# Sixteen transposes in a row: regrouping the softmax transposes and score matmuls of a hybrid attention block

## The chip, the cores and the metric

One core of a Trainium2 chip runs the whole program. The metric is device time in microseconds (us) per execution, smaller is better. Engines named below: PE (TensorE, matmuls; PEld are its weight loads), DVE (VectorE), ACT (ScalarE), SP (which issues the DMAs). Each engine runs its own instructions strictly in the order in which they stand, and waits on semaphores for the others.

## The reference

One layer of a diffusion backbone over 512 latent tokens of width 1024 and 256 context tokens, all in 32-bit floats. After modulation and RMSNorm one large input projection feeds a gated short convolution and a neighbourhood attention of 16 heads of width 64; both branches are projected, merged through sigmoid gates, projected again, normalised and added to `x`. The part that the change touches is the attention:

```
s_nb  = einsum(q_r, k_win) * scale + bias      # window of keys around each query
s_ctx = einsum(q_r, k_ctx) * scale             # all 256 context keys
p     = softmax(concatenate([s_nb, s_ctx]))
out   = einsum(p_nb, v_win) + einsum(p_ctx, v_ctx)
```

## The kernel before

**Precision.** Every fp32 operand is split into a high part H (rounded to the matmul's fp32r format) and a low part L = x - H; a product is made of two or three matmuls (`split`, L67 to L71: ACT writes H, DVE writes L). A *unit* (`unit`, L227) is one 128x512 output of the input projection: 24 matmuls on PE. Units of values (`proj_N`) and of context (`proj_c`) are 16 matmuls each.

**The attention stage** runs over 8 pairs of heads, 2 heads a pair, 4 blocks of 128 queries a head: 64 blocks. For each block `scores` (L540) makes 128 x 512 scores in one PSUM bank (2 to 4 matmuls, L551 or L560), DVE adds the bias and takes the row maximum (L567) and negates it (L571), ACT takes the exponential and its row sum (L574) into a tile `pt`, DVE inverts the sum (L575) and scales `pt` (L576). PE then turns `pt` by four 128x128 transposes into another bank (`turn2`, L579, matmuls at L583), and ACT and DVE split that into TH and TL (L70, L71). When all four blocks of a head are turned, `gather` (L587, 12 matmuls at L599) multiplies by the values; ACT copies half of the result to `tmp` (L604), and DVE adds it into `attn` (L605, L606).

**Fill.** PE has far more to do in this stage than attention: `plan` (L162) gives each pair a list of projection work, 6 to 8 pieces of about one unit or two value units each: queries and keys of the next pair (`keys_queries`: a unit of queries with rotary embedding, a unit of keys, the context's keys), values, convolution, gates. The loop from L664 spreads these pieces evenly over the pair's eight blocks. DVE and ACT evacuate each piece: `rope` (L481 to L490), the query splits (L516, L518), the key splits (L527, L528), the weight splits (tile `w`, L70, L71, two of each per chunk of weights).

**Order and banks.** In a pass of the loop come: the fill, at block 0 the `gather` of the head before, the scores of the block that is two further on, and at every second block the transposes of two blocks, 8 in a row. Scores rotate over PSUM banks 3 and 4, transposes over 5 and 6, gathers use 7, fill units 0 to 2 (L474, L659). The framework's scheduler keeps mostly to this order, but may pull single instructions forward.

Of the kernel before, what the change touches and what calls it, by code (L numbers as in the profile page):

```python
# [9 lines left out]
F32 = mybir.dt.float32  # L10
# [5 lines left out]
P = 128  # L16
D = 1024
KT = 8
S = 512
C = 256  # L20
EPS = 1e-6
NPAIR = 8
# [5 lines left out]
def layer(ctx: ExitStack, tc, xp, ctxt, cc, wmod, small, wfirst, win, wout, wo, rel, tab, out):  # L28
# [5 lines left out]
    cv = ctx.enter_context(tc.tile_pool(name="cv", bufs=2))  # L34
# [20 lines left out]
    def pairs(tag, n, dtype=F32R):  # L55
        t = [hp.tile([P, 2, n], dtype, name=f"{tag}{k}") for k in range(KT)]
        return t, ([x[:, 0] for x in t], [x[:, 1] for x in t])
# [6 lines left out]
    _, hx = pairs("h", S)  # L64
    hcs, hc = pairs("hc", C)

    def split(H, L, src, scale=None):  # L67

        if scale is None:
            nc.scalar.copy(H, src)  # L70
            nc.vector.tensor_sub(L, src, H.bitcast(F32))  # L71
        else:
            nc.scalar.mul(H, src, scale)
            nc.vector.scalar_tensor_tensor(
                out=L, in0=src, scalar=scale, in1=H.bitcast(F32), op0=ALU.mult, op1=ALU.subtract
            )
# [156 lines left out]
    with ExitStack() as p0:  # L233
# [8 lines left out]
        tps = Banks(6, 7)  # L242
# [228 lines left out]
    aw = pa.enter_context(tc.tile_pool(name="aw", bufs=2, reuse_waits="tile"))  # L471
    swap = [(i + 16) % 32 for i in range(32)]
    lo, hi = slice(0, 64), slice(64, P)
    psS, psT, psO = Banks(3, 4), Banks(5, 6), Banks(7)  # L474
    bt = aw.tile([P, 5, 256], F32, name="bt", bufs=1)
    nc.vector.memset(bt[:, 4], 0.0)
    V, KQ = {}, {}
# [62 lines left out]
    def scores(p, h, b):  # L540
        qd, qe, ks = KQ[p]
        if b == 0:
            nc.sync.dma_start(bt[:, 2 * h:2 * h + 2], rel[p, h])
        s = psS()
        qs = slice(b * P, (b + 1) * P)
        if b < 3:

            t = ks[h][:, b * P:(b + 2) * P]
            kt = bass.AP(t.tensor, t.offset, [t.ap[0], [(4 - b) * P, 2], [1, 2 * P]])
            for n, lhs in enumerate((qd[h], qe[h])):  # L550
                nc.tensor.matmul(  # L551
                    s.rearrange("p (a c) -> p a c", a=2), lhsT=lhs[:, qs], rhs=kt, start=n == 0, stop=n == 1
                )
        else:
            kt = ks[h].rearrange("p (t c) -> p t c", c=P)
            s4 = s.rearrange("p (t c) -> p t c", c=P)
            n = 0
            for lhs in (qd[h], qe[h]):
                for o, i in ((slice(0, 2), slice(0, 4, 3)), (slice(2, 4), slice(4, 6))):
                    nc.tensor.matmul(  # L560
                        s4[:, o], lhsT=lhs[:, qs], rhs=kt[:, i], start=n == 0, stop=n == 3, skip_group_check=True
                    )
                    n += 1
        e = 2 * h + (b == 3)
        m = aw.tile([P, 1], F32, name="m", bufs=4)
        s3 = s.rearrange("p (a c) -> p a c", a=2)
        nc.vector.tensor_tensor_reduce(  # L567
            out=s3, in0=s3, in1=bt[:, e::4 - e][:, 0:2], scale=1.0, scalar=-3.0e38,
            op0=ALU.add, op1=ALU.max, accum_out=m,
        )  # L570
        nc.vector.tensor_scalar(out=m, in0=m, scalar1=-1.0, scalar2=None, op0=ALU.mult)  # L571
        pt = aw.tile([P, S], F32, name="pt", bufs=3)
        z = aw.tile([P, 1], F32, name="z", bufs=4)
        nc.scalar.activation(pt, s, AF.Exp, bias=m, scale=1.0, accum_out=z)  # L574
        nc.vector.reciprocal(z, z)  # L575
        nc.vector.tensor_scalar(out=pt, in0=pt, scalar1=z, scalar2=None, op0=ALU.mult)  # L576
        return pt

    def turn2(pts, b, TH, TL):  # L579
        tps = [psT().rearrange("p (c q) -> p c q", c=4) for _ in pts]  # L580
        for tp, pt in zip(tps, pts):
            for c in range(4):
                nc.tensor.transpose(tp[:, c], pt[:, c * P:(c + 1) * P], ident)  # L583
        for n, tp in enumerate(tps):
            split(TH[:, b + n], TL[:, b + n], tp)

    def gather(p, h, TH, TL):  # L587
        r, q = (lo, hi)[h], (hi, lo)[h]
        o = psO()
        o3 = o.rearrange("p (b q) -> p b q", b=4)  # L590

        work = [(4, slice(0, 4), lambda t: t[:, :, 2]), (5, slice(0, 4), lambda t: t[:, :, 3])]
        work.append((0, slice(0, 4, 3), lambda t: t[:, 0:4:3, 0]))
        for k in range(1, 3):
            work.append((k, slice(k - 1, k + 1), lambda t, k=k: t.rearrange("p b c q -> p (b c) q")[:, 4 * k - 3:4 * k + 1:3]))
        work.append((3, slice(2, 4), lambda t: t[:, 2:4, 1]))
        for n, (kt, dst, src) in enumerate(work):
            for t in (TH, TL):
                nc.tensor.matmul(  # L599
                    o3[:, dst], lhsT=V[p][:, kt, h], rhs=src(t),  # L600
                    start=n == 0 and t is TH, stop=n == len(work) - 1 and t is TL,
                )
        tmp = aw.tile([P, S], F32, name="tmp", bufs=1)
        nc.scalar.copy(tmp[r], o[q])  # L604
        nc.vector.tensor_add(attn[p][r, 64:512], o[r, :448], tmp[r, :448])  # L605
        nc.vector.tensor_add(attn[p][r, 0:64], o[r, 448:], tmp[r, 448:])  # L606
# [29 lines left out]
    def chain(*gs):  # L636
        for g in gs:
            yield from g
# [10 lines left out]
    fill = []  # L649
# [7 lines left out]
            }[name](i))  # L657
        fill.append(f)
    pj.tags = (0, 1, 2)  # L659
    blocks = [(p, h, b) for p in range(NPAIR) for h in range(2) for b in range(4)]  # L660
    pts = {n: scores(*blocks[n]) for n in range(2)}
    T = None
    done = 0
    for i, (p, h, b) in enumerate(blocks):  # L664
        slot = i % 8
        if slot == 0:
            items = chain(*(g for g, _ in fill[p]))
            total, done = sum(n for _, n in fill[p]), 0
        upto = -(-total * (slot + 1) // 8)
        while done < upto:  # L670
            next(items)
            done += 1
        if T is not None and b == 0:
            gather(*T)
        if i + 2 < len(blocks):
            pts[i + 2] = scores(*blocks[i + 2])
        if b == 0:
            TH = aw.tile([P, 4, 4, P], F32R, name="TH", bufs=1)
            TL = aw.tile([P, 4, 4, P], F32R, name="TL", bufs=1)
            T = p, h, TH, TL  # L680

        if b % 2:
            turn2([pts.pop(i - 1), pts.pop(i)], b - 1, TH, TL)
    gather(*T)
    for _ in gate2(3):
        pass
# [23 lines left out]
    for j in range(KT):  # L710
        w = chunk()
        g = G[j]
# [9 lines left out]
        if j == 5:  # L722

            gpost = bp.tile([P, D], F32, name="gpost")
            for i in range(2):
                gb = cv.tile([P, S], F32, name="ta")
                ps = pj()
                for k in range(4):
                    n = 4 * i + k
# [147 lines left out]
```

## Time and profile before

| | |
|---|---|
| median of 3 runs | 731.56 us (730.94 to 731.61) |
| the profiled execution | 731.4 us, its span 729.6 us |
| granted TensorE clock, mean | 0.999 |
| PE busy | 718.8 us (99%) |
| DVE busy | 513.9 us (70%) |
| ACT busy | 332.6 us (46%) |
| transposes L583 | 256, mean 272 ns each from start to end |
| scores' exponentials L574 | 64, mean 693 ns each |

The span is from the first to the last instruction of the profiled execution. Matmuls are pipelined: the next starts before the last has ended, so what one costs is the distance between starts, not its duration. The attention stage lies between 139 and 516 us of the span.

### The profile page before, as it was taken

The page shows a single profiled execution, that of the slowest core. Times are in us where ns is not written, and L with a number is a line of the kernel's source. Part 1 is how long each engine was busy: PE and PEld are TensorE (multiplying, and loading weights), DVE is VectorE, ACT ScalarE, POOL GpSimd, SP SyncE. Part 2 cuts the span into 40 slices and gives each one's busy share as a digit, 9 for nine tenths or more (in the row PEclk, how much of TensorE's full clock was granted, in tenths as well). Part 3 has the DMA queues.
Part 4 walks back from the last instruction along what each step waited for, and adds up shares of the span by engine and source line. Part 5 has one row for each costly group of instructions (what it writes and reads, how often), then busy time and mean ns, then how long its engine had stood idle before and what let it go on. Part 6 is the DMA issues. An engine that isn't in the chain of part 4 may idle for free.

```text
span 729.6 us, 9373 instructions
## 1 busy us (share of the span) xinstructions
PE 718.8 (99%) x3526; PEld 603.3 (83%) x3526; DVE 513.9 (70%) x1057; ACT 332.6 (46%) x619; POOL 0.7 (0%) x6
## 2 busy tenths in 40 slices
PE   7999999999999999999999999999999999999996
PEld 4888888888888888888888888888888888888886
DVE  6979999796998968879879779675753324334423
ACT  6565433563565544654546436434723213314321
POOL 0000000000000000000000000000000000000000
PEclk9999999999999999999999999999999999999999
DMA  8966873213122122122322212222132232234503
GB/s 344 405 244 206 306 263 106 88 55 118 58 73 73 64 81 74 58 74 71 116 73 73 72 59 73 85 77 84 58 115 90 85 115 93 81 116 154 192 2 114
DMA packets 25678, 85.57 MB, mean 117 GB/s; under 512 B 2977, under 2 KB 3361, under 8 KB 25634
## 3 DMA queue, kind: packets, MB, share of 16 engines
q1 hardware_dynamic: 25490, 84.79, 33.8%
q8 instruction: 27, 0.44, 0.2%
q10 hardware_dynamic: 144, 0.20, 0.1%
q14 instruction: 17, 0.14, 0.1%
HBM read 82.88 MB, written 2.10 MB: 116 GB/s over the span
## 4 chain that ended last, share of the span: by engine, by line
PE 94%; DVE 2%; ACT 1%; DMA 1%; SPq 0%; issue 0%; DVEq 0%; ACTq 0%
PE ps L115 20%; PE ps L117 20%; PE ps L116 20%; PE ps L128 6%; PE ps L754 6%; PE ps L599 4%; PE ps L583 4%; PE ps L132 3%; PE ps L551 3%; PE ps L140 2%; PE ps L315 2%; PE ps L319 2%; PE ps L316 2%; DMA wm<-in_wmod 1%; PE ps L560 1%; PE ps L144 1%
## 5 line engine op out<-in xcount | busy, mean ns | idle before, releaser
L115 PE MATMUL ps<-h,w 128*128 128x512 f32 x528 | 207.7, 393 | 0.0
L117 PE MATMUL ps<-h,w 128*128 128x512 f32 x528 | 205.9, 390 | 0.0
L116 PE MATMUL ps<-h,w 128*128 128x512 f32 x528 | 205.8, 390 | 0.0
L71 DVE TENSOR_TENSOR w<-raw,w 128x1024 fp32r<-128x1024 f32 (+1 forms) x98 | 113.3, 1173 | 61.4 <-ACT w L70 61.2
L70 ACT CAST w<-raw 128x1024 fp32r<-128x1024 f32 (+1 forms) x98 | 96.7, 1017 | 85.2 <-PE ps L117 65.7
L117 PEld LDWEIGHTS ps<-h,w 128*128 128x128 f32 x528 | 99.1, 188 | 20.9
L116 PEld LDWEIGHTS ps<-h,w 128*128 128x128 f32 x528 | 99.2, 188 | 20.1
L115 PEld LDWEIGHTS ps<-h,w 128*128 128x128 f32 x528 | 99.2, 188 | 20.0
L574 ACT ACTIVATE pt<-ps,m 128x512 f32<-128x512 f32 x64 | 44.3, 693 | 59.5 <-DVE m L571 59.5
L567 DVE CUSTOM_DVE_ANT_1 ps<-ps,bt 128x512 f32<-128x512 f32 x56 | 38.6, 700 | 15.1 <-PE ps L551 12.0
L71 DVE TENSOR_TENSOR TL<-ps,TH 128x512 fp32r<-128x512 f32 x64 | 42.7, 680 | 5.2 <-ACT TH L70 5.2
L128 PE MATMUL ps<-w,h 128*128 128x512 f32 x128 | 45.2, 395 | 0.0
L70 ACT CAST TH<-ps 128x512 fp32r<-128x512 f32 x64 | 35.0, 588 | 6.6 <-PE ps L583 6.4
L714 DVE SCALAR_TENSOR_TENSOR g<-g,ps 128x512 f32<-128x512 f32 x16 | 11.0, 686 | 37.6 <-PE ps L117 37.6
L632 ACT ACTIVATE g<-ps 128x512 f32<-128x512 f32 x16 | 9.6, 598 | 59.3 <-PE ps L117 59.3
L132 PE MATMUL ps<-w,h 128*128 128x256 f32 x128 | 36.0, 281 | 0.0
L583 PE MATMUL ps<-ident,pt 128*128 128x128 f32 x256 | 33.3, 272 | 0.0
L576 DVE TENSOR_SCALAR pt<-pt,z 128x512 f32<-128x512 f32 x64 | 30.8, 482 | 1.0
L583 PEld LDWEIGHTS ps<-ident,pt 128*128 128x128 f32 x256 | 29.4, 140 | 2.2
L516 ACT ACTIVATE qd<-ta 64x512 fp32r<-64x512 f32 x32 | 20.2, 631 | 22.4 <-DVE ta L490 14.2
L599 PE MATMUL ps<-TH,V 128*128 128x256 f32 (+1 forms) x96 | 28.5, 319 | 0.0
L128 PEld LDWEIGHTS ps<-w,h 128*128 128x128 f32 x128 | 24.0, 187 | 5.3
(156 smaller groups left out, 1192.5 us busy)
## 6 DMA issues: line engine op xcount, KB each, us to landing
raw<-in_win SPq DMA_DIRECT2D x74, 512.0 KB, 4.3
wm<-in_wmod SPq DMA_DIRECT2D x34, 512.0 KB, 7.1
raw<-in_wout SPq DMA_DIRECT2D x16, 512.0 KB, 4.3
bt<-in_rel SPq DMA_DIRECT2D x16, 256.0 KB, 2.6
raw<-in_wo SPq DMA_DIRECT2D x8, 512.0 KB, 4.9
fraw<-in_wfirst SPq DMA_DIRECT2D x8, 384.0 KB, 8.2
x<-in_xp SPq DMA_DIRECT2D x4, 512.0 KB, 5.1
xr<-in_xp SPq DMA_DIRECT2D x4, 512.0 KB, 6.9
```

Of the source, the lines that this page charges most:

```text
L70: nc.scalar.copy(H, src)
L71: nc.vector.tensor_sub(L, src, H.bitcast(F32))
L115: nc.tensor.matmul(ps, lhsT=H[:, k, cs], rhs=mH[k], start=k == 0, stop=False)
L116: nc.tensor.matmul(ps, lhsT=H[:, k, cs], rhs=mL[k], start=False, stop=False)
L117: nc.tensor.matmul(ps, lhsT=L[:, k, cs], rhs=mH[k], start=False, stop=k == KT - 1)
L128: nc.tensor.matmul(ps, lhsT=mH[k][:, ts], rhs=both[:, k].rearrange("p a c -> p (a c)"), start=k == 0, stop=False, skip_group_check=True,)
L132: nc.tensor.matmul(ps[:, :256], lhsT=mL[k][:, ts], rhs=H[:, k], start=False, stop=k == KT - 1, skip_group_check=True)
L567: nc.vector.tensor_tensor_reduce(out=s3, in0=s3, in1=bt[:, e::4 - e][:, 0:2], scale=1.0, scalar=-3.0e38, op0=ALU.add, op1=ALU.max, accum_o ...
L574: nc.scalar.activation(pt, s, AF.Exp, bias=m, scale=1.0, accum_out=z)
L583: nc.tensor.transpose(tp[:, c], pt[:, c * P:(c + 1) * P], ident)
L599: nc.tensor.matmul(o3[:, dst], lhsT=V[p][:, kt, h], rhs=src(t), start=n == 0 and t is TH, stop=n == len(work) - 1 and t is TL,)
L754: nc.tensor.matmul(ps, lhsT=mm[m][k][:, ts], rhs=w[k][:, cols], start=k + o == 0, stop=k == KT - 1 and o == 2)
```

## The change

All four blocks of a head are now turned in one row of 16 transposes, over four PSUM banks, two of which are the scores' own (banks 3 and 4). Scores are no longer made two blocks ahead: in each head come one piece of fill, the `gather` of the head before, the scores of blocks 0 and 1, one piece of fill, the scores of blocks 2 and 3, the rest of that head's fill, and then the 16 transposes. `pt` has four buffers in place of three, and the `tmp` of `gather` comes from a pool of two buffers that the rotary embedding, the convolution and the gates use too.

```diff
-    psS, psT, psO = Banks(3, 4), Banks(5, 6), Banks(7)
+    psS, psT, psO = Banks(4, 3), Banks(4, 5, 6, 3), Banks(7)
...
-        pt = aw.tile([P, S], F32, name="pt", bufs=3)
+        pt = aw.tile([P, S], F32, name="pt", bufs=4)
...
-    def turn2(pts, b, TH, TL):
+    def turn(pts, TH, TL):
+
         tps = [psT().rearrange("p (c q) -> p c q", c=4) for _ in pts]
...
-        for n, tp in enumerate(tps):
-            split(TH[:, b + n], TL[:, b + n], tp)
+        for b, tp in enumerate(tps):
+            split(TH[:, b], TL[:, b], tp)
...
-        tmp = aw.tile([P, S], F32, name="tmp", bufs=1)
+        tmp = cv.tile([P, S], F32, name="tb")
...
-    blocks = [(p, h, b) for p in range(NPAIR) for h in range(2) for b in range(4)]
-    pts = {n: scores(*blocks[n]) for n in range(2)}
...
-    for i, (p, h, b) in enumerate(blocks):
...
-        if T is not None and b == 0:
-            gather(*T)
-        if i + 2 < len(blocks):
-            pts[i + 2] = scores(*blocks[i + 2])
-        if b == 0:
+    for p in range(NPAIR):
+        items = chain(*(g for g, _ in fill[p]))
+        total = sum(n for _, n in fill[p])
+        for h in range(2):
+            def run(n):
+                for _ in range(n):
+                    next(items)
+
+            run(1)
+            if T is not None:
+                gather(*T)
+            pts = [scores(p, h, b) for b in (0, 1)]
+            run(1)
+            pts += [scores(p, h, b) for b in (2, 3)]
+            run((total + 1 - h) // 2 - 2)
             TH = aw.tile([P, 4, 4, P], F32R, name="TH", bufs=1)
             TL = aw.tile([P, 4, 4, P], F32R, name="TL", bufs=1)
             T = p, h, TH, TL
-
-        if b % 2:
-            turn2([pts.pop(i - 1), pts.pop(i)], b - 1, TH, TL)
+            turn(pts, TH, TL)
```

PE in the first head of pair 3, before: the scores of block 3 (ps_2765), then the eight transposes of blocks 0 and 1 (pt_2614, pt_2625), then the context's keys (ps_2792).

```order
L560 MATMUL ps_2765<-ks_2296,qd_2254 128x256 x2
L560 MATMUL ps_2765<-ks_2296,qe_2256 128x256 x2
L583 MATMUL ps_2778<-ident_71,pt_2614 128x128 x4
L583 MATMUL ps_2779<-ident_71,pt_2625 128x128 x4
L140 MATMUL ps_2792<-hc0_88,w_2522 128x512
```

The same head in the change: the scores of blocks 2 and 3, the context's keys (ps_2776) and two value units (the last is ps_2835) behind them, then the row of transposes.

```order
L551 MATMUL ps_2752<-ks_2283,qd_2231 128x512
L551 MATMUL ps_2752<-ks_2283,qe_2233 128x512
L560 MATMUL ps_2763<-ks_2283,qd_2231 128x256 x2
L560 MATMUL ps_2763<-ks_2283,qe_2233 128x256 x2
...
L132 MATMUL ps_2835<-w_2625,h7_87 128x256
L584 MATMUL ps_2861<-ident_71,pt_2695 128x128 x4
L584 MATMUL ps_2862<-ident_71,pt_2706 128x128 x4
L584 MATMUL ps_2863<-ident_71,pt_2758 128x128 x4
L584 MATMUL ps_2864<-ident_71,pt_2771 128x128 x4
```

Blocks 2 and 3 now have the context's keys and two value units between their scores and their transposes; before, a block's scores stood two blocks ahead of the loop, and blocks 0 and 1 alone were turned here.

DVE in that same head, before: from the negated maximum of block 3 (m_2770) over the splits of TL, the sum of the rotary embedding of the keys (ta_2755), the scaling of the block (pt_2773), to the key splits (ks).

```order
L571 TENSOR_SCALAR m_2770<-m_2770 128x1
L71 TENSOR_TENSOR TL_2723<-ps_2778,TH_2722 128x512
L486 TENSOR_TENSOR ta_2755<-ta_2755,tb_2757 128x512
L575 RECIPROCAL z_2774<-z_2774 128x1
L71 TENSOR_TENSOR TL_2723<-ps_2779,TH_2722 128x512
L576 TENSOR_SCALAR pt_2773<-pt_2773,z_2774 128x512
L151 TENSOR_TENSOR ta_2809<-ta_2809,ps_2792 128x256
L528 TENSOR_TENSOR ks_2728<-ta_2755,ks_2728 64x512
L528 TENSOR_TENSOR ks_2729<-ta_2755,ks_2729 64x512
L528 TENSOR_TENSOR ks_2728<-ta_2809,ks_2728 64x256
L528 TENSOR_TENSOR ks_2729<-ta_2809,ks_2729 64x256
```

And in the change, from the maximum of block 3 (ps_2763) to the scalings of blocks 2 and 3 (pt_2758, pt_2771):

```order
L567 ISA ps_2763,m_2768<-ps_2763,bt_1041 128x512
L567 ISA m_2768 128x1
L486 TENSOR_TENSOR ta_2742<-ta_2742,tb_2744 128x512
L571 TENSOR_SCALAR m_2768<-m_2768 128x1
L151 TENSOR_TENSOR ta_2793<-ta_2793,ps_2776 128x256
L71 TENSOR_TENSOR w_2804<-raw_2800,w_2804 128x4x256
L528 TENSOR_TENSOR ks_2715<-ta_2742,ks_2715 64x512
L528 TENSOR_TENSOR ks_2716<-ta_2742,ks_2716 64x512
L575 RECIPROCAL z_2759<-z_2759 128x1
L575 RECIPROCAL z_2772<-z_2772 128x1
L528 TENSOR_TENSOR ks_2715<-ta_2793,ks_2715 64x256
L576 TENSOR_SCALAR pt_2758<-pt_2758,z_2759 128x512
L576 TENSOR_SCALAR pt_2771<-pt_2771,z_2772 128x512
```

The two scalings now stand behind a weight split and three of the four key splits; before, the one scaling stood ahead of them, and the weight split further back.

PE in the first head of pair 1, in the change: the end of the context's keys (ps_1886), the transposes of blocks 0 and 1 (pt_1805, pt_1816), then 26 matmuls of value units (ps_1951, ps_1975), and the transposes of blocks 2 and 3 in their midst.

```order
L144 MATMUL ps_1886<-hc7_95,w_1611 128x256
L584 MATMUL ps_1912<-ident_71,pt_1805 128x128 x4
L584 MATMUL ps_1913<-ident_71,pt_1816 128x128 x4
L128 MATMUL ps_1951<-w_1735,h0_80 128x512
...
L132 MATMUL ps_1975<-w_1735,h4_84 128x256
L584 MATMUL ps_1914<-ident_71,pt_1868 128x128 x4
L584 MATMUL ps_1915<-ident_71,pt_1881 128x128 x4
L128 MATMUL ps_1975<-w_1735,h5_85 128x512
```

In that head the row of 16 is split in two by the scheduler, since only the context's keys remain as fill behind the scores of blocks 2 and 3.

## Rows read from the trace of the kernel before

**Rows 1.** Busy time by engine in the attention stage (stretch, length, busy and count).

```profile
139.00:516.00 377.00, 376.61 (x1966) 321.35 (x1965) 302.81 (x714) 193.35 (x393) 0.00 (x0) 1.00 0.23 75
```

**Rows 2.** What PE waited for in that stage (total, times, longest, us).

```profile
PE ps L551 <- ACT pt L574: 0.4, 1, 0.4
```

**Rows 3.** Timeline of PE, 311 to 325 us (start, duration, instruction, count).

```profile
311.71 1.03 PE L583 MATMUL ps<-ident,pt 128*128 128x128 f32 x8
312.50 0.48 PE L115 MATMUL ps<-h,w 128*128 128x512 f32 x1
312.82 0.40 PE L116 MATMUL ps<-h,w 128*128 128x512 f32 x1
...
315.13 0.39 PE L117 MATMUL ps<-h,w 128*128 128x512 f32 x1
...
318.53 0.39 PE L115 MATMUL ps<-h,w 128*128 128x512 f32 x1
...
323.97 0.39 PE L551 MATMUL ps<-ks,qd 128*128 128x512 f32 x1
```

**Rows 4.** Timeline of PE around its one wait of the stage.

```profile
202.18 0.40 PE L128 MATMUL ps<-w,h 128*128 128x512 f32 x1
202.97 0.50 PE L551 MATMUL ps<-ks,qd 128*128 128x512 f32 x1 [0.39 <-ACT pt L574]
```

**Rows 5.** Timeline of ACT there.

```profile
202.72 0.19 ACT L574 ACTIVATION_READ_ACCUMULATOR pt<-ps,m 128x1 f32 x1
```

**Rows 6.** Timeline of PE, first head of pair 3: gather, scores, context, values, transposes.

```profile
278.48 0.39 PE L599 MATMUL ps<-TH,V 128*128 128x512 f32 x1
...
280.34 0.40 PE L551 MATMUL ps<-ks,qd 128*128 128x512 f32 x1
...
287.52 0.48 PE L140 MATMUL ps<-hc,w 128*128 128x512 f32 x1
...
290.43 0.40 PE L551 MATMUL ps<-ks,qd 128*128 128x512 f32 x1
...
296.44 0.39 PE L551 MATMUL ps<-ks,qd 128*128 128x512 f32 x1
...
296.91 0.60 PE L583 MATMUL ps<-ident,pt 128*128 128x128 f32 x4
```

**Rows 7.** Timeline of DVE in the same head.

```profile
278.68 0.69 DVE L481 TENSOR_TENSOR ta<-ps,cosin 128x512 f32<-128x512 f32 x1 [0.63 <-PE ps L117]
...
283.78 0.70 DVE L567 CUSTOM_DVE_ANT_1 ps<-ps,bt 128x512 f32<-128x512 f32 x1
...
284.62 0.15 DVE L571 TENSOR_SCALAR m<-m 128x1 f32<-128x1 f32 x1
...
285.82 0.49 DVE L576 TENSOR_SCALAR pt<-pt,z 128x512 f32<-128x512 f32 x1
286.46 0.69 DVE L481 TENSOR_TENSOR ta<-ps,cosin 128x512 f32<-128x512 f32 x1 [0.15 <-PE ps L117]
...
290.59 0.68 DVE L71 TENSOR_TENSOR TL<-ps,TH 128x512 fp32r<-128x512 f32 x1
291.19 0.68 DVE L486 TENSOR_TENSOR ta<-ta,tb 128x512 f32<-128x512 f32 x1
...
292.45 0.48 DVE L576 TENSOR_SCALAR pt<-pt,z 128x512 f32<-128x512 f32 x1
292.84 0.41 DVE L151 TENSOR_TENSOR ta<-ta,ps 128x256 f32<-128x256 f32 x1
293.29 2.31 DVE L528 TENSOR_TENSOR ks<-ta,ks 64x512 fp32r<-64x512 f32 x4
295.62 0.70 DVE L567 CUSTOM_DVE_ANT_1 ps<-ps,bt 128x512 f32<-128x512 f32 x1
...
296.24 1.22 DVE L71 TENSOR_TENSOR w<-raw,w 128x1024 fp32r<-128x1024 f32 x1
297.38 0.15 DVE L571 TENSOR_SCALAR m<-m 128x1 f32<-128x1 f32 x1
```

More of the change, by code (lines that the diff above doesn't have):

```diff
@@ L659, in layer @@
     pj.tags = (0, 1, 2)
-    blocks = [(p, h, b) for p in range(NPAIR) for h in range(2) for b in range(4)]
-    pts = {n: scores(*blocks[n]) for n in range(2)}
     T = None
-    done = 0
-    for i, (p, h, b) in enumerate(blocks):
[L665 to L672, printed above, removed]
-        if T is not None and b == 0:
-            gather(*T)
-        if i + 2 < len(blocks):
-            pts[i + 2] = scores(*blocks[i + 2])
-        if b == 0:
+    for p in range(NPAIR):
[12 more added lines that the diff above has]
+            run((total + 1 - h) // 2 - 2)
             TH = aw.tile([P, 4, 4, P], F32R, name="TH", bufs=1)
```

## The prediction

> **What bounds the kernel now.** I read the busy time by stage first: in the attention stage, where the whole change lies, PE is busy for 376.61 of 377.00 us at a granted clock of 1.00, DVE for 302.81, ACT for 193.35 [rows 1]. So PE's stream of matmuls is the time, and any other engine counts only where it makes PE wait. The waits come next: PE waits once there, 0.4 us [rows 2]. As busy PE may still lose time between starts, I read the starts last. In a plain unit 24 matmuls take 318.53 to 323.97, 5.44 us or 0.227 each [rows 3]; that is the pitch to which the rest is held. The change issues the same matmuls and the same evacuations. It can shorten the time only by what PE loses at the borders between kinds of matmul and in that wait, and lengthen it without limit where PE must wait for `pt`.
>
> **Borders of the transposes.** Eight transposes last 1.03 us from the first start to the last end, one lasts 0.27 (the table), so seven steps take 0.76, 0.11 each. From the first transpose to the second matmul behind them is 311.71 to 312.82, 1.11 us: eight times 0.11 and one matmul of 0.227 make 1.11. Changing over is thus free. The ten matmuls behind run at 0.231 (312.82 to 315.13), 0.04 us over plain pitch [rows 3]. A run of transposes costs some 0.04 us beyond its work. The order has 33 such runs before and 17 in the change: 16 x 0.04 = 0.65 us gone.
>
> **Borders of the scores.** Two matmuls of a block's scores take 0.47 us (296.44 to 296.91) [rows 6] against 0.454 at plain pitch: 0.016 a run, and no more than that behind it. The order has 57 runs of scores before, 33 in the change: 24 x 0.02 = 0.45 us. Together 1.1 us, bounds 0 (if the lag belongs to the transposes themselves, whose number stays) and 1.5.
>
> **The one wait.** At 202.18 a matmul starts and the next only at 202.97, where 0.23 would do: 0.56 us; the matmul after comes about 0.1 late as well. The score matmul waited for its bank, until the exponential's row sum ended at 202.72 + 0.19 = 202.91, and started 0.06 us later [rows 4, 5]. In the change, scores follow each other in pairs with a unit between, so this wait goes: 0.66 us.
>
> **What is late next: `pt` of blocks 2 and 3.** In the first head of pair 3 the last scaling before its transposes starts at 292.45 and ends at 292.93; its four transposes start at 296.91 + 4 x 0.11 = 297.35 [rows 6, 7]. So the cover was 4.4 us. In the change, both later blocks lie one stretch behind their scores. In each first head of pairs 0 to 6 that stretch also holds the query and key work of the next pair, so I lay PE and DVE side by side from the end of the query unit (time 0; 278.48 in the trace).
>
> PE: gather 1.86 (278.48 to 280.34), two pairs of scores 0.94, unit 5.44, scores 0.94, context's keys 2.82 (287.52 to 290.43 is 2.91, of which 0.09 belongs to the transposes ahead), one more unit 5.44 (value units 290.90 to 296.44, 5.54) [rows 6, 3]. Transposes start at 17.44; block 2 is due after eight of them at 18.32, block 3 at 18.76 (0.1 later in pairs 3 and 5).
>
> DVE, in its new order, by distances between starts [rows 7]: the rotary embedding of the queries starts at 0.20; with the sums into `attn` and the query split it takes 5.10 (278.68 to 283.78): 5.30. Two bias sums at 0.62 (295.62 to 296.24): 6.54. From a negation to its scaling 1.20 (284.62 to 285.82): 7.74; the second exponential is 0.69 long and lies behind the first, so the second scaling starts at 8.42, and the next instruction 0.40 later: 8.82. The start of the keys' embedding, a bias sum, the second query split, a product and a negation take 4.13 (286.46 to 290.59): 12.95. The second bias sum 0.62: 13.57. Sum of the embedding and small ones, 290.59 to 292.45 without the two TL splits of 0.60 that have moved: 0.66, and one negation more, 0.07: 14.30. The context's sum 0.45 (292.84 to 293.29): 14.75. A weight split 1.14 (296.24 to 297.38): 15.89. Three of the four key splits: of 2.31 I give the last and short one 0.44, so 1.87: 17.76. An inversion 0.07: 17.83. Scaling of block 2 to 18.32, of block 3 to 18.71. With the 0.06 of rows 5: 18.38 and 18.77.
>
> So `pt` comes at 18.38 where PE is due at 18.32. The cover of 4.4 us has shrunk to nothing, within the error of the sum. For pairs 2 to 6 I take 0.1 us of wait each: 0.5. In pair 1 only the context's keys stand behind the scores; the order puts 26 value matmuls ahead of blocks 2 and 3: 17.44 - 5.44 + 0.88 + 26 x 5.54 / 32 + 0.09 = 17.47, a wait of 0.9. In pair 0 there is neither gather (PE is due 1.86 earlier) nor sum into `attn` (0.8 less for DVE), and the first exponential's wait, some 0.85 of the 1.20 (less a negation of 0.15 and an inversion), lies beside the embedding: 18.38 - 1.65 = 16.73 against 16.46, a wait of 0.3. Waits in all 1.7 us. Bounds: none at all if DVE is 0.9 faster than my sum; and another full step from negation to scaling, 1.20, late in all seven heads, 8.4 us more.
>
> **Costed at nothing.** The second heads have a whole unit (5.44) behind the scores and little but two bias sums, two exponentials and two scalings in it (1.24 + 0.07 + 1.20 + 0.68 + 0.5 = 3.7 us): 1.7 us of cover, and two transposed blocks more. The gather waits for four splits after the last transposes (4 x 0.60 and the first cast, some 3 us) and has a unit of 5.44 in front. Scores of the next head need banks 3 and 4 back from those splits, later still. Scores of block 2 need the first exponential's end at 7.5, due 8.24; of block 3 at 8.2, due 8.71. The shared `tmp` rotates over two buffers, and the user two back is over by a unit each time; without that cover ACT would stand for about one 0.7 us product. SP's queue has its DMAs in the same sequence.
>
> **Sum.** 731.4 - 1.1 - 0.66 + 1.7 = 731.3, and the median of the runs stands 0.16 above the profiled execution: 731.5 us.
>
> **Rivals.**
>
> *DVE is later than my sum, and PE waits in every first head.* For: my margin is 0.06 us, ACT's part in it (casts of keys and weights between the two exponentials, and a copy that waits for the context's unit ahead of the third exponential) is only followed roughly, and each 0.1 us is paid in seven heads, 0.7 us. Against: DVE runs ahead whenever a second head leaves it idle, so lateness doesn't pile up from head to head. It decides the sign from 18.6 on for the scaling of block 2; with 0.5 us more than my sum the time is 731.5 + 7 x 0.5 = 735.0.
>
> *The waits don't come.* If DVE is 0.9 us quicker than my sum in these heads, PE never waits: 731.56 - 1.76 = 729.8. If it is 0.4 quicker, only pair 1 waits, 0.5: 730.3, which counts with the forecast. For: overlaps of neighbouring instructions may be better than in the rows I added. Against: I took the closest rows there are.
>
> *The regrouping doesn't save what it is credited with.* The lag behind transposes may belong to each transpose, whose number stays. Then only the 0.66 us goes: 732.6.
>
> *The clock falls behind the longer row.* In the trace the stage has a granted clock of 1.00, the level of 2.4 GHz, with rows of eight [rows 1]; no row of sixteen is in it. A unit at half the clock would take 5.44 us more; sixteen of them 87 us: 818. The rule behind it: the Trainium skill, "TensorE: Matmul & The Clock Gate", Part 4, says that transposes don't count as PE-busy the way other matmuls do, which speaks against a longer row of them; by that rule alone this rival would come nearer. The trace bears it out no further than this: with 33 runs of transposes it shows no fall.
>
> **How the numbers follow.** A measurement of this kernel can tell 0.2% from no change, 1.46 us: faster is below 730.10, slower above 733.02. Forecast 0.44, inside; the regrouping without its saving 0.12, inside; PE waiting in every first head 0.30, slower; no waits 0.12, faster; the clock 0.02, slower. So faster 0.12, same 0.56, slower 0.32. The range: 729.8, no waits, to 735.0, 0.5 us more in seven heads; the likeliest case alone 730.3 to 732.8.
>
> **What would show it.** Right: PE's busy time in the stage about as before; a wait of transposes for the scaling of `pt` of near 0.9 us in the first head of pair 1 and of 0.3 or less in the others; the wait of the score matmul gone; the clock at 1.00. Wrong: waits of half a microsecond or more in the first heads of pairs 2 to 6, or scores waiting for the exponentials, or gathers for TL; on the other side, no wait at all and units behind transposes at plain pitch from the first matmul on.

## The result, and the profile after

The changed kernel takes 734.11 us (median of 6 runs, 733.38 to 734.34) against 731.65 (730.94 to 731.96) for the kernel before, run beside it: ratio 1.0036, 95% interval 1.0026 to 1.0046. It is 2.5 us slower; the prediction said 731.5, no change that could be told. The ratios here leave out single executions far off the others, none of them profiled: of the kernel before one of 1471.61 and one of 1471.69 us at a granted clock of 1.00, and of e5 below one of 902.14 us at 0.755.

The profiled execution took 734.34 us, its span is 732.4. I read the same views as before. Busy time by stage of the changed kernel first (stretch, length, then busy time and count of PE, its weight loads, DVE, ACT and POOL, granted clock, DMA share, GB/s); the stage now ends at 520, so the stretch is two microseconds longer than in [rows 1]:

```profile
139.00:518.00 379.00, 377.50 (x1965) 321.20 (x1965) 304.74 (x713) 191.87 (x392) 0.00 (x0) 1.00 0.22 74
```

PE idles 1.50 us here, where it idled 0.39, and the clock stands at 1.00, the level of 2.4 GHz, as before. The waits of PE in the changed kernel (total, times, longest, us):

```profile
PE ps L362 <- ACT crow L334: 3.4, 1, 3.4
PE ps L584 <- DVE pt L576: 1.2, 2, 1.1
PE ps L395 <- ACT x L358: 1.1, 1, 1.1
PE ps L315 <- ACT h L70: 0.3, 1, 0.3
```

The score matmul's wait for ACT [rows 2] is gone. In its place transposes (L584) wait for the scaled `pt`, longest in pair 1. PE there, in the changed kernel (start, duration, instruction, count):

```profile
206.53 0.40 PE L128 MATMUL ps<-w,h 128*128 128x512 f32 x1
206.77 0.28 PE L132 MATMUL ps<-w,h 128*128 128x256 f32 x1
208.11 0.96 PE L584 MATMUL ps<-ident,pt 128*128 128x128 f32 x7 [1.06 <-DVE pt L576]
```

And DVE beside it:

```profile
205.34 1.40 DVE L528 TENSOR_TENSOR ks<-ta,ks 64x512 fp32r<-64x512 f32 x2
206.77 0.22 DVE L575 RECIPROCAL z<-z 128x1 f32<-128x1 f32 x2
207.03 0.42 DVE L528 TENSOR_TENSOR ks<-ta,ks 64x256 fp32r<-64x256 f32 x1
207.48 0.88 DVE L576 TENSOR_SCALAR pt<-pt,z 128x512 f32<-128x512 f32 x2
```

The last value matmul starts at 206.77, the transposes at 208.11 where 206.88 was due: 1.23 us. DVE works through three key splits until the first of the two scalings can start at 207.48.

That wait is the only one which the view of waits shows at its size. The others hide inside a row of transposes, since instructions with the same name are shown as one. In a second head, where `pt` is early, the row of 16 and what follows is this (PE, changed kernel):

```profile
324.52 1.91 PE L584 MATMUL ps<-ident,pt 128*128 128x128 f32 x16
326.18 0.48 PE L115 MATMUL ps<-h,w 128*128 128x512 f32 x1
326.50 0.40 PE L116 MATMUL ps<-h,w 128*128 128x512 f32 x1
...
328.77 0.39 PE L117 MATMUL ps<-h,w 128*128 128x512 f32 x1
```

A row that waits for nothing lasts 1.91 us. In the first head of pair 3 it lasts 2.10. Below are the start of that head's gather, the row, and DVE's two scalings beside it (PE first, then DVE, changed kernel):

```profile
279.10 0.39 PE L600 MATMUL ps<-TH,V 128*128 128x512 f32 x1
...
291.09 0.40 PE L128 MATMUL ps<-w,h 128*128 128x512 f32 x1
...
296.75 2.10 PE L584 MATMUL ps<-ident,pt 128*128 128x128 f32 x16
298.60 0.48 PE L128 MATMUL ps<-w,h 128*128 128x512 f32 x1
```

```profile
296.44 0.22 DVE L575 RECIPROCAL z<-z 128x1 f32<-128x1 f32 x2
296.70 0.42 DVE L528 TENSOR_TENSOR ks<-ta,ks 64x256 fp32r<-64x256 f32 x1
297.15 0.88 DVE L576 TENSOR_SCALAR pt<-pt,z 128x512 f32<-128x512 f32 x2
```

The first scaling ends at 297.63 by its own record, the ninth transpose starts at 297.78. Taken start to start, the ninth transposes of the seven first heads come late by 0.13, 1.23, 0.31, 0.16, 0.31, 0.16 and 0.32 us (pairs 0 to 6): 2.6 us in all, which is the loss, nearly.

The rest must be looked for in the pitch. The same 32 value matmuls in the first head of pair 3 take 5.55 us before, from 290.89 to the scores at 296.44 [rows 6]:

```profile
290.89 0.39 PE L128 MATMUL ps<-w,h 128*128 128x512 f32 x1
...
296.33 0.28 PE L132 MATMUL ps<-w,h 128*128 128x256 f32 x1
```

and 5.66 in the changed kernel, from 291.09 to 296.75, with no wait in either. A value matmul of 512 columns lasts 399 ns in the mean of the changed kernel's stage, 393 before; a unit's (L115) 393 against 395 (groups by line: count, busy us, mean ns), the changed kernel first and the kernel before second:

```profile
L115 PE MATMUL ps<-h,w 128*128 128x512 f32 x322 | 126.7, 393 | 0.0
...
L128 PE MATMUL ps<-w,h 128*128 128x512 f32 x96 | 34.3, 399 | 0.0
```

```profile
L115 PE MATMUL ps<-h,w 128*128 128x512 f32 x324 | 128.1, 395 | 0.0
...
L128 PE MATMUL ps<-w,h 128*128 128x512 f32 x96 | 33.9, 393 | 0.0
```

So units got a little quicker, as predicted, and value work slower, which nobody had asked for. From the first context matmul to the last gather, 398.13 us became 400.73. Of that, gaps of more than 0.1 us beyond the pitch make 0.78 before and 2.85 now; without them 397.35 became 397.87. But the two stretches don't hold the same work: among the matmuls of the last gather stand three unit matmuls before and four now. PE there, the kernel before first, then the changed one:

```profile
514.51 0.50 PE L599 MATMUL ps<-TH,V 128*128 128x512 f32 x1
...
515.56 0.39 PE L599 MATMUL ps<-TL,V 128*128 128x512 f32 x1
```

```profile
517.31 0.50 PE L600 MATMUL ps<-TH,V 128*128 128x512 f32 x1
...
518.58 0.40 PE L600 MATMUL ps<-TL,V 128*128 128x512 f32 x1
```

With one pitch of 0.23 us added for that one matmul, the kernel before has 397.58: the pitch lost 0.3 us.

### The profile page after: what moved, and what is told of

It is laid out like the page before. It is cut to its first block, busy times and chain, and to the rows that moved or that the text cites. A ratio compares the mean times of both kernels' runs of the same rounds, so it can differ in the third digit from the quotient of the medians.

```text
span 732.4 us, 9405 instructions
## 1 busy us (share of the span) xinstructions
PE 720.3 (98%) x3526; PEld 603.5 (82%) x3526; DVE 516.5 (71%) x1057; ACT 331.7 (45%) x619; POOL 0.7 (0%) x6
## 4 chain that ended last, share of the span: by engine, by line
PE 87%; DVE 9%; DMA 1%; ACT 1%; issue 1%; SPq 0%; DVEq 0%; ACTq 0%
PE ps L115 19%; PE ps L116 19%; PE ps L117 19%; PE ps L751 6%; PE ps L128 6%; PE ps L584 4%; PE ps L600 3%; PE ps L132 3%; PE ps L551 2%; PE ps L315 2%; PE ps L319 2%; PE ps L316 2%; DVE qe L518 2%; DVE ps L567 1%; DMA wm<-in_wmod 1%; PE ps L140 1%
## 5 line engine op out<-in xcount | busy, mean ns | idle before, releaser
L115 PE MATMUL ps<-h,w 128*128 128x512 f32 x528 | 207.1, 392 | 0.0
L115 PEld LDWEIGHTS ps<-h,w 128*128 128x128 f32 x528 | 99.2, 188 | 19.9
L71 DVE TENSOR_TENSOR TL<-ps,TH 128x512 fp32r<-128x512 f32 x64 | 40.5, 680 | 3.5 <-ACT TH L70 3.4
L132 PE MATMUL ps<-w,h 128*128 128x256 f32 x128 | 35.9, 280 | 0.0
L584 PE MATMUL ps<-ident,pt 128*128 128x128 f32 x256 | 31.8, 273 | 1.5 <-DVE pt L576 1.2
L70 ACT CAST TH<-ps 128x512 fp32r<-128x512 f32 x64 | 33.1, 602 | 0.0
L584 PEld LDWEIGHTS ps<-ident,pt 128*128 128x128 f32 x256 | 28.7, 140 | 4.8 <-ACT TH L70 1.4
```

The lines of the kernel that those rows point to most:

```text
L115: nc.tensor.matmul(ps, lhsT=H[:, k, cs], rhs=mH[k], start=k == 0, stop=False)
L132: nc.tensor.matmul(ps[:, :256], lhsT=mL[k][:, ts], rhs=H[:, k], start=False, stop=k == KT - 1, skip_group_check=True)
```

## The experiments

Theory after the result: the loss is the waits for `pt` of block 2, one to one, and the regrouping gives back nothing of what the waits cost. Rivals: the regrouping saves its 1.1 us and some other thing costs it again; or waits take no time that would not be lost elsewhere. All times below are medians beside the kernel before at 731.44 (e1 to e4) and 731.51 (e5 to e8). A time is longer than its span, by 1.77 to 1.84 us in the mean of most kernels' runs, but by 2.15 to 2.18 in e1, e6 and e7. No profile shows what lies there, and it isn't the stage, so the median span is given beside the time where it matters: 729.6 us for the kernel before (729.7 beside e5 to e8), 732.3 for the changed one (732.4 in e4).

**e1, scores of all four blocks in one group.** The waits are taken away by an earlier position of the scores of blocks 2 and 3; the row of 16 stays.

```diff
-    psS, psT, psO = Banks(4, 3), Banks(4, 5, 6, 3), Banks(7)
+    psS, psT, psO = Banks(4, 5, 6, 3), Banks(4, 5, 6, 3), Banks(7)
...
-            pts = [scores(p, h, b) for b in (0, 1)]
-            run(1)
-            pts += [scores(p, h, b) for b in (2, 3)]
-            run((total + 1 - h) // 2 - 2)
+            pts = [scores(p, h, b) for b in range(4)]
+            run((total + 1 - h) // 2 - 1)
```

> All four blocks' scores of a head are issued in one group behind the gather, over the four banks that the transposes use too; the row of 16 transposes stays. Theory A (the loss is PE waiting in the first heads for the scaling of pt of block 2, some 2.6 us in all, and borders between kinds of matmul cost nothing either way): the scores stand a whole unit earlier, so no transpose waits any more; 731.5 us, 2.6 below the changed kernel, level with the kernel before or up to 0.3 us under it. Theory B (the loss comes from the row of 16 itself and from the neighbours it now has): the waits go but the time stays at 733 us or more. Theory C (scores, not transposes, are what matters: fewer runs of scores save as the prediction had it, 0.02 us a run): 731.5 less 17 x 0.02 and less, 731.0.

Measured: 732.03 us, ratio 1.0009 (1.0000 to 1.0018). No transpose waits for `pt`; the waits of PE in this kernel are those of other stages:

```profile
PE ps L362 <- ACT crow L334: 3.3, 1, 3.3
PE ps L395 <- ACT x L358: 0.6, 1, 0.6
PE ps L315 <- ACT h L70: 0.3, 1, 0.3
```

The 2.6 us of waits went, and 2.1 us of time with them; the span fell by 2.5, from 732.4 to 729.9, and 0.36 of the time lies outside it. The time is nearest to theory A (731.5). But with fewer borders than any other kernel here (16 runs of scores, 16 of transposes) and no wait, it is still not below the kernel before. Its stage without gaps is 398.22 us, 0.6 above the 397.58 of the kernel before for the same work.

**e2, the same with two rows of 8.** Against e1; not shown is that `turn` is also told the number of its first block.

```diff
-            run((total + 1 - h) // 2 - 1)
+            run((total + 1 - h) // 2 - 2)
...
-            turn(pts, TH, TL)
+            turn(pts[:2], TH, TL, 0)
+            run(1)
+            turn(pts[2:], TH, TL, 2)
```

> As e1, but the transposes stand in two rows of 8 with one piece of fill between them, 32 runs in place of 16. If a run of transposes costs 0.04 us beyond its work, as the prediction had it, 0.65 us slower than e1; if borders are free, within 0.2 us of e1 and no transpose waits.

Measured: 731.78 us, ratio 1.0006 (0.9997 to 1.0015), not slower than e1 with twice as many rows of transposes. The prediction's price of 0.04 us a row would have made 0.65. By spans it is 0.1 above e1 (730.0 against 729.9), with 0.4 more of gaps. One wait came back, at pair 1 (0.53 by starts; the view names the inversion, and the transpose starts 0.15 us after the scaling behind it):

```profile
PE ps L584 <- DVE z L575: 0.4, 1, 0.4
```

**e3, DVE made later on purpose.** Two halvings of a part of the bias tile that holds zeros (0.28 us each) stand ahead of block 3's bias sum in the seven first heads; they leave the zeros, so the result stays the same.

```diff
+        if h == 0 and b == 3 and p < 7:
+            for _ in range(2):
+                nc.vector.tensor_scalar(out=bt[:, 4], in0=bt[:, 4], scalar1=0.5, scalar2=None, op0=ALU.mult)
```

> The changed kernel with two small instructions of DVE more (a quarter of a microsecond each, half a microsecond together) ahead of the bias sum of block 3 in each of the seven first heads that also carry query and key work; the result is not touched. Theory A: the scaling of pt comes 0.5 us later there and PE waits for it 0.5 us longer in each head, 3.5 us in all, 737.6 us, less what the scheduler pulls into the gap (four matmuls of the next unit, 0.9 us, stand ahead of the last transposes in some heads). Theory B: the time does not move by more than 0.5 us.

Measured: 742.93 us, ratio 1.0154 (1.0140 to 1.0169), 8.8 above the changed kernel, where the added instructions last 14 x 0.28 = 3.9. Its waits:

```profile
PE ps L587 <- DVE pt L579: 9.8, 7, 1.6
```

The gaps are 11.27 us in all, 8.4 more than in the changed kernel, and the time rose 8.8: about one to one. That it is more than the dose has its reason on DVE, where the order changed: block 3's scaling now stands behind both weight splits (w, 1.23 and 1.21 us) instead of beside block 2's. DVE of this kernel, first head of pair 2:

```profile
250.75 0.49 DVE L579 TENSOR_SCALAR pt<-pt,z 128x512 f32<-128x512 f32 x1
251.27 0.42 DVE L528 TENSOR_TENSOR ks<-ta,ks 64x256 fp32r<-64x256 f32 x1
251.73 1.23 DVE L71 TENSOR_TENSOR w<-raw,w 128x1024 fp32r<-128x1024 f32 x1
252.87 0.15 DVE L578 RECIPROCAL z<-z 128x1 f32<-128x1 f32 x1
252.94 1.21 DVE L71 TENSOR_TENSOR w<-raw,w 128x1024 fp32r<-128x1024 f32 x1
254.06 0.48 DVE L579 TENSOR_SCALAR pt<-pt,z 128x512 f32<-128x512 f32 x1
```

and PE, whose last four transposes start at 254.69, when that scaling is done:

```profile
252.70 0.40 PE L117 MATMUL ps<-h,w 128*128 128x512 f32 x1
254.69 0.63 PE L587 MATMUL ps<-ident,pt 128*128 128x128 f32 x4 [1.60 <-DVE pt L579]
```

So the dose is not a clean one; only the relation of waits to time is read from it.

**e4, the changed kernel again**, beside e1 to e3; no edit.

> The changed kernel once more on the same chip as e1 to e3, for the comparison: 734.1 us, the waits of its seven first heads again 0.1, 1.2, 0.3, 0.2, 0.3, 0.2, 0.3 us, 2.6 us in all.

Measured: 734.14 us, ratio 1.0036 (1.0023 to 1.0049). The seven gaps are 0.14, 1.21, 0.32, 0.15, 0.32, 0.16 and 0.31: they belong to the kernel, not to the execution.

**e5 to e7, value work in single pieces.** To give pair 1 a piece of fill ahead of its transposes, the six value units are handed out one by one, in the changed kernel (e5), the kernel before (e6) and e2 (e7).

```diff
-            if t % 2:
-                yield
+            yield
...
-                "qk": (lambda i: (keys_queries(i), 3)), "v": (lambda i: (values(i), 3)),
+                "qk": (lambda i: (keys_queries(i), 3)), "v": (lambda i: (values(i), 6)),
```

> The changed kernel, with the value work handed out in 6 single pieces instead of 3 pairs, so that the first heads find one more piece of fill between the scores of the last two blocks and the row of 16 transposes. Theory (the loss is the 2.61 us of waits at that row plus about 0.35 us in the pitch of the matmuls): the wait of pair 1 shrinks from 1.22 to about 0.2, those of pairs 3 and 5 go, together 1.3 to 1.5 us less than the changed kernel, about 732.7. Rival (the waits only hide time that TensorE would lose elsewhere, in slower weight loads between the products): the same 734.1 with the waits gone. If more changes between units cost by themselves: up to 1 us above the changed kernel.

> The kernel before, with the value work handed out in 6 single pieces instead of 3 pairs, nothing else. Theory: its one wait of 0.67 us at pair 1 goes, and the order of the rest stays, so 730.8 to 731.0 against 731.5. Rival (the pitch of the value units depends on what comes ahead of them): a change of up to 1 us either way without any wait. If the first holds, this kernel beats both.

> The kernel of e2 (scores of all four blocks in one group, two rows of 8 transposes with one piece of fill between) with the value work handed out in 6 single pieces. Theory: its wait of 0.53 us at pair 1 goes, 731.2 to 731.4. Rival (the pitch of the value units): 731.8 or up to 732.5 with no wait.

Measured: 735.11, 732.31 and 732.75 us, ratios 1.0052 (1.0038 to 1.0066), 1.0015 (1.0006 to 1.0024) and 1.0019 (1.0010 to 1.0028). The theory's numbers failed in all three: each kernel became 0.8 to 1.0 us slower. The wait at which the edit aimed went or shrank, and others came. In e5 transposes of pair 1 are late by 0.16 instead of 1.23, but gathers and scores now wait for TL (waits of PE, e5):

```profile
PE ps L599 <- DVE TL L71: 0.6, 2, 0.3
PE ps L550 <- DVE TL L71: 0.5, 1, 0.5
PE ps L583 <- DVE pt L575: 0.3, 2, 0.2
```

In e6 the score matmul no longer waits, and transposes of pair 1 do, since a weight split stands ahead of the scaling (DVE, e6):

```profile
208.27 1.20 DVE L71 TENSOR_TENSOR w<-raw,w 128x1024 fp32r<-128x1024 f32 x1
209.39 0.48 DVE L575 TENSOR_SCALAR pt<-pt,z 128x512 f32<-128x512 f32 x1
```

In e7 a gather waits for TL (waits of PE, e7):

```profile
PE ps L599 <- DVE TL L71: 0.8, 1, 0.8
```

The gaps grew by 0.93, 0.53 and 0.53 us, the time by 0.97, 0.80 and 0.97, and the span, without what lies outside it, by 0.9, 0.5 and 0.6. So the gaps are the loss here too. The stage without gaps is 0.22 longer in e6 and 0.24 in e7, from one profile each; two profiles of the changed kernel differ by 0.17.

**e8, only the row of 16 undone.** Scores in pairs and shared banks stay; blocks 0 and 1 are turned one piece earlier (`turn` is again told its first block, not shown).

```diff
-            run((total + 1 - h) // 2 - 2)
+            run((total + 1 - h) // 2 - 3)
...
-            turn(pts, TH, TL)
+            turn(pts[:2], TH, TL, 0)
+            run(1)
+            turn(pts[2:], TH, TL, 2)
```

> The changed kernel with the row of 16 transposes alone undone: the transposes of blocks 0 and 1 go one piece of fill earlier as a row of 8, those of blocks 2 and 3 stay at the end; the scores in pairs and the shared banks stay. Theory (borders between transposes and products cost nothing, the waits are those for the scaled probabilities of block 2): 733.8 to 734.4, with waits as in the changed kernel (2.6 us) at the second row. The prediction's term for the borders (17 runs against 33, 0.65 us): 734.8.

Measured: 734.43 us, ratio 1.0042 (1.0028 to 1.0055), 0.3 above the changed kernel: at the edge of the theory's expectation (734.4), and less than the 734.8 of the prediction's price. With 0.2 less of gaps, its stage without them is, for the same work, 0.3 to 0.5 longer than in the two profiles of the changed kernel. Here, unlike in e2, twice as many rows seem to cost something, half of the prediction's 0.65 or more, though the two profiles of the changed kernel are 0.17 apart themselves.

**All kernels side by side.** Runs of scores and of transposes (counted in the traces), gaps over 0.1 us beyond the pitch, and the stage (first context matmul to last gather) less these gaps, from one profile each; then the medians of span and time. In the kernels before, e6, e8, e2 and e7 the stage holds one unit matmul less than in the others, as shown above; 0.23 us is added to theirs.

| kernel | scores | transposes | gaps us | stage less gaps us | span us | time us |
|---|---|---|---|---|---|---|
| before | 57 | 33 | 0.78 | 397.58 | 729.6 | 731.5 |
| e6 | 58 | 32 | 1.31 | 397.79 | 730.2 | 732.31 |
| changed | 33 | 17 | 2.85 | 397.87 | 732.3 | 734.11 |
| e4, changed again | 33 | 17 | 2.86 | 398.04 | 732.4 | 734.14 |
| e5 | 33 | 16 | 3.78 | 398.18 | 733.3 | 735.11 |
| e3 | 33 | 24 | 11.27 | 398.06 | 741.15 | 742.93 |
| e8 | 33 | 33 | 2.64 | 398.37 | 732.6 | 734.43 |
| e1 | 16 | 16 | 0.24 | 398.22 | 729.9 | 732.03 |
| e2 | 16 | 32 | 0.64 | 398.10 | 730.0 | 731.78 |
| e7 | 16 | 32 | 1.17 | 398.34 | 730.6 | 732.75 |

The span follows the gaps. The stage less gaps doesn't fall with the number of borders: the two kernels with most of them are the lowest. No kernel here beats the one before.

## Why the prediction was wrong

**The step that failed first: the saving of 1.1 us, from "a run of transposes costs some 0.04 us beyond its work" and 0.02 us a run of scores.** The lag is there, and behind transposes it did shrink: in the whole units behind them, beyond a pitch of 0.2266, it is 0.68 us in 20 units before and 0.24 in 12 units now (0.32 in the second profile, e4). Scores and the units behind them lost only 0.1 less, where I had 0.45 (24 x 0.02 is 0.48, besides). Together that is 0.5 us saved. But a lag isn't a property of that border. A unit of 24 matmuls loses 0.00, 0.01, 0.02, 0.03 or 0.05 us according to what stood ahead of it: units behind the context's keys lose nothing in the changed kernel and 0.05 in e1. And value work got slower by 0.5 us, as the 5.55 and 5.66 us above show, the rest (gaps under 0.1 us in and behind waiting rows, keys, gathers) by 0.3. That makes 0.3 lost, and the stage less its gaps says the same (397.58 to 397.87). So 0.3 us is lost where I had 1.1 saved: 1.4 of error. I priced one kind of border from the ten matmuls behind it in one place and let the price vanish with the border. The rival that the regrouping saves nothing, which I gave 0.12, was right on this part, and too kind. A doubled number of rows changes the stage less gaps by -0.1 us in e2 against e1 and by +0.3 to +0.5 in e8 against the changed kernel: no price that goes with a row as such.

**The waits for `pt`: right in kind and place, 2.6 us where I had 1.7.** Pair 1 has 1.23 (0.9), pair 0 0.13 (0.3), pairs 2, 4 and 6 0.31, 3 and 5 0.16 (0.1 each). Two terms were small. I took 0.06 us from the end of an engine's work to the matmul that waits, from ACT's row [rows 4, 5]; from the end of the scaling to the transpose it is 0.15 in all seven heads. Part of it stood in [rows 4]: the waiting matmul lasts 0.50 and the next came 0.1 late, which I had counted once, on the other side. And the sum of DVE's instructions was 0.2 short: in pair 3 the first scaling ends 18.53 us after the gather's start (297.63 - 279.10) and not 18.32. PE, too, is 0.1 later there than I had it (296.75 - 279.10 = 17.65 against 17.54), which takes back half of that; what is left is the release, 0.09 longer than I took, and 0.1 of DVE. The rival that DVE is later by half a microsecond in every head, 735.0, didn't come about; its sign did. e1 and e3 show that these waits are the time: 2.6 us of them less is 2.5 of span less (2.1 of time), 8.4 more is 8.8 more.

**What held.** The score matmul's wait of 0.66 is gone. Second heads have at least 3.3 us from the last scaling to its transposes (I had 1.7 and the two blocks ahead, 0.9). Gathers and scores don't wait for TL or the exponentials in the changed kernel. The copy into the shared `tmp` still waits for the gather's matmuls alone, 35.9 us in all against 35.7 before, so the shared pool costs nothing there. The clock stays at 1.00 through the rows of 16 transposes in the profiled execution's stage, and is 0.997 to 0.999 over the span in all six, so that rival didn't come about. On that rule of the Trainium skill ("TensorE: Matmul & The Clock Gate", Part 4, that transposes don't count as PE-busy): no profile here, with rows of 8 or of 16 between units, shows a fall that would come of it.

**The sum.** Gaps at the transposes +2.6, the score matmul's wait -0.67, the pitch +0.3, gaps in the last gather +0.1: 2.4 us for the stage, of the 2.5 between the medians. Of my error of 2.6 (731.5 to 734.11), 1.4 is the saving and 0.9 the waits; 0.1 is the kernel before, which ran that much higher beside it, 0.1 the last gather, and 0.1 I can't assign. That 734.11 lies within the stated range (729.8 to 735.0) is luck: its upper end stood for half a microsecond more of wait in each of seven heads, and most of the error is the saving.

**What stays open.** Why a stretch of value work runs at 0.347 us a pair of matmuls in some places and at 0.354 in others, with the same operands and no wait. Ahead of the quick stretches mostly stand two score matmuls or a row of transposes, ahead of the slow ones the context's keys or four and more score matmuls; but in e1 and e2 some stretches behind transposes are slow as well. The order of the instructions alone doesn't decide it: the 32 value matmuls behind the row of 16 in pair 5 take 5.63 us in the first profile of the changed kernel and 5.73 in the second, the first profile first:

```profile
398.04 0.48 PE L128 MATMUL ps<-w,h 128*128 128x512 f32 x1
...
403.67 0.39 PE L600 MATMUL ps<-TH,V 128*128 128x512 f32 x1
```

```profile
397.59 0.48 PE L128 MATMUL ps<-w,h 128*128 128x512 f32 x1
...
403.32 0.40 PE L600 MATMUL ps<-TH,V 128*128 128x512 f32 x1
```

No run here separates what does. Nor was the new pool of `tmp`, the fourth buffer of `pt` or the sharing of banks 3 and 4 undone by itself.

## What to carry to other kernels

When PE is busy 99% of a stage, a lag of tens of nanoseconds behind a border is not a saving until the same work has been timed behind what will stand there instead. A wait of the busy engine for another, though, was paid in full here: where work is moved so that the consumer is due at the very time of the producer, price the wait as certain, with the time from the producer's end to the consumer's start taken from the whole of the row, and multiply it by every head. More fill between them is no sure help either: it moves the other engine's work too, and with it the wait.

## What the hardware showed that I had not expected

From the end of DVE's scaling to the start of the transpose that waits for it, 0.15 us in every one of seven heads of the changed kernel, the same in its second profile, and the same at every waiting transpose of e2, e3, e5, e6 and e8. A row of 16 transposes that waits for nothing costs its work and no more: from its start to the second matmul behind it 1.98 us (324.52 to 326.50), 16 x 0.109 and one pitch of 0.227. The pitch of matmuls without any wait is not one number: 5.55 or 5.66 us for the same 32 in two kernels, and 5.63 or 5.73 for one stretch of one kernel in two executions.
